# How a recurrence's operands reach TensorE: loads as the data lie and a spread by ScalarE, two chunks to a transpose, one buffer in another order

## The chip, the cores and the metric

The kernel runs on one core of one Trainium2 chip. The metric is the time of one execution on the device in microseconds (us), as a median of several runs. The engines are TensorE (PE, with its weight loads listed as PEld), VectorE (DVE), ScalarE (ACT), GpSimd (POOL) and SyncE (SP), whose queue issues nearly all DMAs of this kernel.

## The reference

One decoder layer over 2048 tokens of width 1024. After a norm and one input projection, two causal mixers run side by side: a diagonal state-space mixer, and RWKV-7 time mixing with 8 heads of 64. Their outputs are joined by an output projection, and a squared-ReLU MLP follows. The change touches the second mixer alone, whose recurrence the reference computes token by token:

```python
    def step(state, inp):
        r_t, d_t, k_t, v_t, kk_t, a_t = inp
        sa = jnp.einsum('bhvk,bhk->bhv', state, -kk_t)
        state = (state * d_t[:, :, None, :]
                 + sa[..., None] * (kk_t * a_t)[:, :, None, :]
                 + v_t[..., None] * k_t[:, :, None, :])
        return state, jnp.einsum('bhvk,bhk->bhv', state, r_t)
```

## The kernel before

The kernel does not step through tokens. It cuts the 2048 tokens into 32 chunks of 64, four chunks to a batch of 256 tokens, eight batches. Two heads share the 128 partitions, so there are four head pairs (`NP`), and a batch has four *units* and four *values*, one for each pair. The input phase leaves six operands for each pair and batch in DRAM, in `f_dram`, in the order k, v, b, a, q, bv, 256 numbers a partition each.

- `units` (L806) loads b and a of one pair into `ba`, a, q and k into `aq`, multiplies them chunk by chunk on TensorE (`ps_b` L817, `ps_a` L826) and evicts the products to `bQ` (VectorE L821, ScalarE L822) and `aR` (VectorE L827, ScalarE L828). `ba` holds a block diagonal: the first head's 64x64 block stands in the upper left, the second head's in the lower right, and the rest was set to zero once (L775). `load_pair` (L800) fills the two blocks straight from DRAM, one DMA for each half of the partitions, in runs of 64 numbers.
- After the fourth unit of a batch, `bQ`'s 32x32 diagonal blocks go to the DRAM buffer `abd` (L832), in the order row, quarter, block, column. `invert` (L861) reads them back as `M` (L865) with one block to a partition, inverts them in 62 small VectorE instructions (L876, L877) in `Z`, which GpSimd clears first (L868), and stores the result to `zd` (L880). `dtc` (L882) and, in `join` (L884), `lo` (L891) are read from `zd`.
- `values` (L834) does the same with k and v: `load_pair` fills `bk` with both as block diagonals, `ps_k` (L853) is multiplied, and `ps_v` (L851) holds four transposes, one for each chunk of v; because v lies on the diagonal, the transposed chunk is a block diagonal too, and one ScalarE copy (L855) takes all four to `vT`.
- `solve` (L908) makes `ps_pq`, evicts it with two ScalarE copies (L923, L924) to `pq`, and multiplies that into `ps_f` and `ps_h`. `chain` (L939) is the serial part: it takes `vT`, `hj`, `gf` and the state `S` through `ps_s` and stores the output rows `Y` (ScalarE L958).

In the main loop, one step handles one chunk of the chain, the solve of the chunk after next, one unit (13 ahead) and one value (5 ahead). TensorE's order is written out by hand there. The order on the other engines and on SyncE's queue is fixed when the kernel is built, by a planner that simulates the engines and takes instructions when their operands are ready in that simulation. Every engine then works through its queue in that order. The buffers `ba`, `aq`, `bk` and `qi` are there twice (`NB`), and `ps_k` and `ps_v` share one PSUM bank. The first two batches' units and inversions run beside the input phase, which ends at about 653 us.

Of the kernel before, what the change touches and what calls it, by code (L numbers as in the profile page):

```python
# [7 lines left out]
F32 = mybir.dt.float32  # L8
# [748 lines left out]
def rwkv_phase(K, f_dram, e_dram, n_dram, y_dram, ntok=2048):  # L757
# [7 lines left out]
    with ExitStack() as st:  # L765
# [5 lines left out]

        bas, aqs = [T([P, 2, NCH, P], f"ba{i}") for i in range(NB)], [T([P, 4, NCH, 64], f"aq{i}") for i in range(NB)]
        ist = c["ist"].rearrange("p (o x) -> p o x", o=1)
        for i in range(NB):
            g.memset(bas[i], 0.0)  # L775
            v.tensor_copy(aqs[i][:, 2], bc(ist, [P, NCH, 64]))
        S = None
# [3 lines left out]
        def begin(b):  # L781
            ub = uns[b % 4]
            B = dict(aR=ub.tile([P, NCH, NP, P], F32, tag="aR", name="aR"),
                     bQ=ub.tile([P, NCH, NP, 192], F32, tag="bQ", name="bQ"),
                     abd=K.dram.tile([32, 4, 16, 32], F32, tag="abd", bufs=3, name="abd"),
                     zd=K.dram.tile([32, 4, 16, 32], F32, tag="zd", bufs=3, name="zd"))

            nr, n2 = un.tile([NCH * NP, P], F32, tag="nr", name="nr"), ub.tile([P, NCH * NP], F32, tag="n2", name="n2")
            nc.sync.dma_start(out=nr, in_=n_dram[b * NCH:(b + 1) * NCH].rearrange("c t h s -> (c t) (h s)"))
            ps = pp("ps_nt")[:, 0:NCH * NP]  # L790
            pe.transpose(out=ps, in_=nr, identity=K.ident[0:NCH * NP, 0:NCH * NP])
            v.tensor_scalar(out=n2, in0=ps, scalar1=1e-24, scalar2=None, op0=ALU.max)
            v.reciprocal(out=n2, in_=n2)
            B["n2"] = n2
            return B
# [3 lines left out]

        def load_pair(t, b, p, o):  # L800

            for h in range(2):
                hp = slice(h * 64, h * 64 + 64)
                nc.sync.dma_start(out=t[hp, :, :, hp].rearrange("p n c x -> p (n c) x"), in_=f_dram[p, hp, b, o:o + 2].rearrange("p n (c x) -> p (n c) x", x=64))

        def units(b, B, p):  # L806

            aR, bQ = B["aR"], B["bQ"]
            i = (b * NP + p) % NB
            ba, aq = bas[i], aqs[i]  # L810
            load_pair(ba, b, p, RW["b"])
            nc.sync.dma_start(out=aq[:, 0:2].rearrange("p n c x -> p n (c x)"), in_=f_dram[p, :, b, RW["a"]:RW["a"] + 2])
            nc.sync.dma_start(out=aq[:, 3].rearrange("p c x -> p (c x)"), in_=f_dram[p, :, b, RW["k"]])
            for uu in range(0, NCH, 2):
                psb = pp("ps_b")
                for u in range(2):
                    pe.matmul(psb[:, u * 192:(u + 1) * 192], ba[:, 0, uu + u], aq[:, 0:3, uu + u], start=True, stop=True)  # L817
                for u in range(2):
# [6 lines left out]
            for u in range(NCH):  # L825
                pe.matmul(ps[:, u * P:(u + 1) * P], ba[:, 1, u], aq[:, 2:4, u], start=True, stop=True)  # L826
            v.tensor_tensor(out=aR[:, :, p, 0:64], in0=r4(ps)[:, :, 64:128], in1=mask(c["ma"], NCH), op=ALU.mult)  # L827
            act.copy(out=aR[:, :, p, 64:128], in_=r4(ps)[:, :, 0:64])  # L828
            if p == NP - 1:
                for hq in range(4):  # L830
                    q0 = (hq % 2) * 32
                    nc.sync.dma_start(out=B["abd"][:, hq], in_=bQ[hq * 32:(hq + 1) * 32, :, :, q0:q0 + 32].rearrange("s c p t -> s (c p) t"))  # L832

        def values(b, B, p):  # L834

            if p == 0:
                kv = kvs[b % 2]
                for n, shape in (("kT", [P, NCH, NP, P]), ("vT", [P, NCH, NP, P]), ("qS", [P, NP, TB])):
                    B[n] = kv.tile(shape, F32, tag=n, name=n)
                nc.sync.dma_start(out=B["qS"], in_=f_dram[:, :, b, RW["q"]].rearrange("t p n -> p t n"))  # L840
            kT, vT = B["kT"], B["vT"]
            i = (b * NP + p) % NB
            bk, qi = bks[i], qis[i]
            load_pair(bk, b, p, RW["k"])
            nc.sync.dma_start(out=qi[:, 0].rearrange("p c x -> p (c x)"), in_=f_dram[p, :, b, RW["q"]])
            for n in range(2):
                ps = pk("ps_" + "kv"[n])
                for u in range(NCH):
                    o = ps[:, u * P:(u + 1) * P]
                    if n:  # L850
                        pe.transpose(out=o, in_=bk[:, n, u], identity=K.ident)  # L851
                    else:
                        pe.matmul(o, bk[:, n, u], qi[:, :, u], start=True, stop=True)  # L853
                if n:
                    act.copy(out=vT[:, :, p], in_=r4(ps))  # L855
                else:
                    B["last"] = v.tensor_tensor(out=kT[:, :, p, 0:64], in0=r4(ps)[:, :, 0:64], in1=mask(c["mk"], NCH), op=ALU.mult)
                    act.copy(out=kT[:, :, p, 64:128], in_=r4(ps)[:, :, 64:128])
                    yield

        def invert(B, eng):  # L861

            M = un.tile([P, 32, 32], F32, tag="M", bufs=2, name="M")
            for par in range(2):
                nc.sync.dma_start(out=M[par * 64:par * 64 + 64], in_=B["abd"].rearrange("s q b t -> (q b) s t"))  # L865
            Z, prod = un.tile([P, 16, 32], F32, tag="Z", bufs=2, name="Z"), un.tile([P, 144], F32, tag="prod", name="prod")
            Zf = Z.rearrange("p i t -> p (i t)")
# [15 lines left out]

        def join(B):  # L884

            bQ, dtc = B["bQ"], B["dtc"]
            up, lo = (bt.tile([P, 16, 32], F32, tag=n, bufs=1, name=n) for n in ("up", "lo"))
            v.transpose(out=up.rearrange("p a t -> p (a t)"), in_=dtc.rearrange("p c a t -> p (c a t)"))
            halves = [(h, slice(h * 64, h * 64 + 32)) for h in range(2)]
            for h, hs in halves:  # L890
                nc.sync.dma_start(out=lo[hs].rearrange("s b t -> s (b t)"), in_=B["zd"][:, 2 * h + 1].rearrange("s b t -> s (b t)"))  # L891
            yield
# [86 lines left out]
        vp = pool(name="rwv", bufs=1)  # L979
        bks, qis = [T([P, 2, NCH, P], f"bk{i}", vp) for i in range(NB)], [T([P, 2, NCH, 64], f"qi{i}", vp) for i in range(NB)]  # L980
        for i in range(NB):
            g.memset(bks[i], 0.0)
            v.tensor_copy(qis[i][:, 1], bc(ist, [P, NCH, 64]))
        bt = pool(name="rwbt", bufs=2, side="right")
# [23 lines left out]
        with tc.manual_schedule(engines={mybir.EngineType.PE}):  # L1008
# [14 lines left out]

            for _ in join(Bs[0]):
                pass
# [721 lines left out]
```

## Time and profile before

| | |
|---|---|
| median of 3 runs | 2565.19 us (2565.0 to 2570.68) |
| profiled execution | 2566.72 us, its span 2565.0 us |
| TensorE busy | 2434.8 us, 95% of the span |
| VectorE, ScalarE, GpSimd busy | 1886.5, 1301.6 and 667.4 us (74%, 51%, 26%) |
| mean granted TensorE clock | 0.979 of full speed |
| recurrence with the hand-written order | about 655 to 965 us of the span |

Times in the rows count from the span's first instruction. A row of a timeline gives start, duration, engine, line, operation, output and inputs, and in brackets how long the engine idled before and what ended that. A busy TensorE is not one at its peak, since the ends of its matmuls are modelled and overlap; where a price of a matmul is needed, the distance between starts is the better figure. SPq is SyncE issuing DMAs.

### The profile page before, as it was taken

How to read it: one execution, taken by the hardware profiler on the slowest of the kernel's cores; microseconds unless marked ns; L12 is line 12 of the kernel's file. 1: busy time of each engine (PE TensorE's matmuls, PEld its weight loads, DVE VectorE, ACT ScalarE, POOL GpSimd, SP SyncE). 2: the span in 40 equal slices, each digit the busy share in tenths (PEclk: the TensorE clock that was granted, in tenths of full speed). 3: DMA queues.
4: the chain of work that ended last, by engine and by line, in shares of the span. 5: the costliest groups of instructions: out<-in, count | busy, mean ns of one | idle time of the engine just before them, and what ended most of it. 6: DMA issues, size and time to landing. Idle time of an engine off the chain costs nothing.

```text
span 2565.0 us, 38224 instructions
## 1 busy us (share of the span) xinstructions
PE 2434.8 (95%) x13084; PEld 2020.9 (79%) x13084; DVE 1886.5 (74%) x3326; ACT 1301.6 (51%) x2555; POOL 667.4 (26%) x662
## 2 busy tenths in 40 slices
PE   7999989999898998999899999999989999999998
PEld 6987667787798987888688888888867778877786
DVE  7558897579687868766777668877757777666777
ACT  6355545465454446555476666666653333333334
POOL 1058798711322223231033230322310000000001
PEclk9999989999899998999999999999999999999999
DMA  9656747997777636443457555766577555455545
GB/s 288 214 166 180 223 120 218 255 259 180 182 161 160 137 88 222 145 155 125 160 205 251 208 191 199 239 209 214 186 265 283 187 182 169 161 175 181 169 158 195
DMA packets 541266, 491.49 MB, mean 192 GB/s; under 512 B 187312, under 2 KB 442800, under 8 KB 541072
## 3 DMA queue, kind: packets, MB, share of 16 engines
q1 hardware_dynamic: 539360, 483.54, 60.7%
q0 software_dynamic: 992, 3.67, 0.5%
q8 instruction: 104, 1.70, 0.3%
q10 hardware_dynamic: 720, 1.84, 0.2%
q14 instruction: 90, 0.74, 0.1%
HBM read 303.23 MB, written 180.49 MB: 189 GB/s over the span
## 4 chain that ended last, share of the span: by engine, by line
PE 70%; DVE 12%; DMA 9%; ACT 3%; issue 2%; POOL 2%; SPq 1%; DVEq 0%; POOLq 0%; ACTq 0%
PE ps_ua L1328 13%; PE ps_da L1328 11%; PE ps_ux L1328 7%; PE ps_dx L1328 5%; PE ps_ub L1328 3%; PE ps_db L1328 3%; PE ps_o L433 2%; PE ps_o L435 2%; PE ps_o L434 2%; DMA wraw<-in_w_down 2%; PE ps_z L433 1%; PE ps_z L434 1%; PE ps_z L435 1%; DMA wr<-in_w_in 1%; DVE acc L1620 1%
## 5 line engine op out<-in xcount | busy, mean ns | idle before, releaser
L1624 ACT COPY c<-ps_da 128x512 f32<-128x512 f32 x192 | 106.3, 588 | 259.1 <-PE ps_da L1328 256.9
L1620 DVE TENSOR_TENSOR acc<-acc,c 128x512 f32<-128x512 f32 x192 | 127.3, 689 | 105.0 <-ACT c L1624 104.8
L433 PE MATMUL ps_z<-xh,wh 128*128 128x512 f32 x448 | 184.8, 413 | 16.9 <-DVE zr L617 7.1
L435 PE MATMUL ps_z<-xh,wl 128*128 128x512 f32 x448 | 182.1, 407 | 0.0
L434 PE MATMUL ps_z<-xl,wh 128*128 128x512 f32 x448 | 181.5, 405 | 0.0
L386 POOL TENSOR_TENSOR frs<-frs,mhalf 128x1 f32<-128x1 f32 x16 | 10.4, 650 | 645.0 <-DVE frs L385 645.0
L1425 DVE TENSOR_TENSOR wl<-wraw,wh 128x512 fp32r<-128x512 f32 x124 | 104.4, 843 | 28.2 <-ACT wh L1424 27.9
L433 PEld LDWEIGHTS ps_z<-xh,wh 128*128 128x128 f32 x448 | 87.5, 195 | 41.7 <-DVE zr L617 8.9
L374 ACT CAST hh<-hr 128x512 fp32r<-128x512 f32 x96 | 59.6, 621 | 110.2 <-PE ps_da L1328 81.5
L609 DVE TENSOR_TENSOR wl<-wr,wh 128x1024 fp32r<-128x1024 f32 x56 | 86.1, 1537 | 35.7 <-ACT wh L608 35.4
L433 PE MATMUL ps_o<-woh,ys 128*128 128x512 f32 x256 | 103.0, 403 | 2.5 <-DVE xrow L1225 2.5
L1424 ACT CAST wh<-wraw 128x512 fp32r<-128x512 f32 x124 | 76.1, 616 | 52.8 <-PE ps_ua L1328 34.1
L435 PEld LDWEIGHTS ps_z<-xh,wl 128*128 128x128 f32 x448 | 87.4, 195 | 19.4 <-issue 0.5
L434 PEld LDWEIGHTS ps_z<-xl,wh 128*128 128x128 f32 x448 | 87.6, 196 | 18.7 <-issue 0.9
L434 PE MATMUL ps_o<-wol,ys 128*128 128x512 f32 x256 | 102.1, 400 | 0.0
L435 PE MATMUL ps_o<-woh,ys 128*128 128x512 f32 x256 | 100.7, 396 | 0.0
L913 POOL TENSOR_TENSOR DT<-dtc,cst 128x128 f32<-128x128 f32 x128 | 56.2, 470 | 159.8 <-PE ps_pq L920 107.2
L1291 POOL TENSOR_TENSOR ws<-wraw 128x512 f32<-128x512 f32 x28 | 41.2, 1471 | 200.9 <-DMA hs_d<-hh 72.7
L1474 DVE TENSOR_TENSOR hh<-hs,hh 128x512 fp32r<-128x512 f32 x96 | 79.7, 830 | 14.5 <-ACT hh L1473 13.5
L1620 DVE TENSOR_TENSOR acc<-acc,ps_dx 128x512 f32<-128x512 f32 x128 | 87.5, 684 | 2.9 <-PE ps_dx L1328 1.1
L1473 ACT CAST hh<-hs 128x512 fp32r<-128x512 f32 x96 | 59.7, 622 | 58.4 <-DVE hs L1490 21.3
L1425 DVE TENSOR_TENSOR wl<-ws,wh 128x512 fp32r<-128x512 f32 x93 | 66.8, 721 | 30.5 <-ACT wh L1424 26.0
(693 smaller groups left out, 8159.2 us busy)
## 6 DMA issues: line engine op xcount, KB each, us to landing
hs_d<-hh SPq DMA_DIRECT2D x256, 256.0 KB
hs<-hs_d SPq DMA_DIRECT2D x126, 512.0 KB
wraw<-in_w_up SPq DMA_DIRECT2D x62, 512.0 KB
wr<-in_w_in SPq DMA_DIRECT2D x56, 512.0 KB
hr<-hr_d SPq DMA_DIRECT2D x94, 256.0 KB
hr_d<-c SPq DMA_DIRECT2D x93, 256.0 KB
xrow<-in_x SPq DMA_DIRECT2D x32, 512.0 KB
wraw<-in_w_down SPq DMA_DIRECT2D x14, 1024.0 KB
```

The costliest lines, as they stand in the source:

```text
L374: nc.scalar.copy(out=hi, in_=raw)
L433: K.nc.tensor.matmul(out, lh, rh, start=i == 0, stop=False)
L434: K.nc.tensor.matmul(out, lh, rl, start=False, stop=False)
L435: K.nc.tensor.matmul(out, ll, rh, start=False, stop=i == n - 1)
L609: v.tensor_tensor(out=wl, in0=wr, in1=wh.bitcast(F32), op=ALU.subtract)
L1328: K.nc.tensor.matmul(ps, a[k], b[k], start=start and k + i == 0, stop=k == n - 1 and i == 2, skip_group_check=True)
L1424: act.copy(out=hi, in_=o)
L1425: v.tensor_tensor(out=lo, in0=o, in1=hi.bitcast(F32), op=ALU.subtract)
L1473: act.copy(out=hi, in_=o)
L1474: v.tensor_tensor(out=lo, in0=o, in1=hi.bitcast(F32), op=ALU.subtract)
L1620: add = lambda eng, o, s: eng.tensor_tensor(out=o, in0=o, in1=s, op=ALU.add)
L1624: act.copy(out=t, in_=ps)
```

## The change

Operands are loaded as they lie in DRAM, in whole rows: for a unit b, a and q in one DMA and k in another, into `fu`; for a value k and v in one and q in another, into `fv`. The two blocks of the diagonal are then written by two ScalarE copies (`spread`), into `ba` for a unit and into `bk` (now k alone) for a value. v is transposed from `fv`, two chunks to a transpose; the blocks come out beside each other, and four small ScalarE copies put them into `vT`, whose zeros are set once by GpSimd at the start. The buffer `abd` is stored in the order quarter, block, row, column, so that `M` reads 4 KB runs; the store's side in DRAM becomes runs of 128 bytes. `Z` has one buffer where it had two. The load of `lo` is issued at the end of the previous batch's `join`, for the batch after.

```diff
-        bas, aqs = [T([P, 2, NCH, P], f"ba{i}") for i in range(NB)], [T([P, 4, NCH, 64], f"aq{i}") for i in range(NB)]
+        bas, fus = [T([P, 2, NCH, P], f"ba{i}") for i in range(NB)], [T([P, 5, NCH, 64], f"fu{i}") for i in range(NB)]
...
-                     abd=K.dram.tile([32, 4, 16, 32], F32, tag="abd", bufs=3, name="abd"),
+                     abd=K.dram.tile([4, 16, 32, 32], F32, tag="abd", bufs=3, name="abd"),
...
-        def load_pair(t, b, p, o):
+        def spread(t, src):
 
             for h in range(2):
                 hp = slice(h * 64, h * 64 + 64)
-                nc.sync.dma_start(out=t[hp, :, :, hp].rearrange("p n c x -> p (n c) x"), in_=f_dram[p, hp, b, o:o + 2].rearrange("p n (c x) -> p (n c) x", x=64))
+                act.copy(out=t[hp, ..., hp], in_=src[hp])
...
-            ba, aq = bas[i], aqs[i]
-            load_pair(ba, b, p, RW["b"])
-            nc.sync.dma_start(out=aq[:, 0:2].rearrange("p n c x -> p n (c x)"), in_=f_dram[p, :, b, RW["a"]:RW["a"] + 2])
-            nc.sync.dma_start(out=aq[:, 3].rearrange("p c x -> p (c x)"), in_=f_dram[p, :, b, RW["k"]])
+            ba, fu = bas[i], fus[i]
+            nc.sync.dma_start(out=fu[:, 0:3].rearrange("p n c x -> p n (c x)"), in_=f_dram[p, :, b, RW["b"]:RW["b"] + 3])
+            nc.sync.dma_start(out=fu[:, 4].rearrange("p c x -> p (c x)"), in_=f_dram[p, :, b, RW["k"]])
+            spread(ba, fu[:, 0:2])
...
-                    nc.sync.dma_start(out=B["abd"][:, hq], in_=bQ[hq * 32:(hq + 1) * 32, :, :, q0:q0 + 32].rearrange("s c p t -> s (c p) t"))
+                    nc.sync.dma_start(out=B["abd"][hq].rearrange("b s t -> s b t"), in_=bQ[hq * 32:(hq + 1) * 32, :, :, q0:q0 + 32].rearrange("s c p t -> s (c p) t"))
...
-            bk, qi = bks[i], qis[i]
-            load_pair(bk, b, p, RW["k"])
-            nc.sync.dma_start(out=qi[:, 0].rearrange("p c x -> p (c x)"), in_=f_dram[p, :, b, RW["q"]])
+            bk, fv = bks[i], fvs[i]
+            nc.sync.dma_start(out=fv[:, 0:2].rearrange("p n c x -> p n (c x)"), in_=f_dram[p, :, b, RW["k"]:RW["k"] + 2])
+            nc.sync.dma_start(out=fv[:, 2].rearrange("p c x -> p (c x)"), in_=f_dram[p, :, b, RW["q"]])
+            spread(bk, fv[:, 0])
...
-                        pe.transpose(out=o, in_=bk[:, n, u], identity=K.ident)
...
-                    act.copy(out=vT[:, :, p], in_=r4(ps))
+
+                    for e in range(0, NCH, 2):
+                        pe.transpose(out=ps[:, e * 64:e * 64 + P], in_=fv[:, 1, e:e + 2].rearrange("p c x -> p (c x)"), identity=K.ident)
+                    for h in range(2):
+                        hp = slice(h * 64, h * 64 + 64)
+                        for e in range(2):
+                            act.copy(out=vT[hp, e::2, p, hp], in_=ps[e * 64:e * 64 + 64, 0:2 * P].rearrange("p (c x) -> p c x", c=2)[:, :, hp])
...
-                nc.sync.dma_start(out=M[par * 64:par * 64 + 64], in_=B["abd"].rearrange("s q b t -> (q b) s t"))
-            Z, prod = un.tile([P, 16, 32], F32, tag="Z", bufs=2, name="Z"), un.tile([P, 144], F32, tag="prod", name="prod")
+                nc.sync.dma_start(out=M[par * 64:par * 64 + 64], in_=B["abd"].rearrange("q b s t -> (q b) s t"))
+            Z, prod = un.tile([P, 16, 32], F32, tag="Z", bufs=1, name="Z"), un.tile([P, 144], F32, tag="prod", name="prod")
...
+        def load_lo(B):
+            B["lo"] = bt.tile([P, 16, 32], F32, tag="lo", bufs=1, name="lo")
+            for h, hs in halves:
+                nc.sync.dma_start(out=B["lo"][hs].rearrange("s b t -> s (b t)"), in_=B["zd"][:, 2 * h + 1].rearrange("s b t -> s (b t)"))
+
+        def join(B, after):
...
-            for h, hs in halves:
-                nc.sync.dma_start(out=lo[hs].rearrange("s b t -> s (b t)"), in_=B["zd"][:, 2 * h + 1].rearrange("s b t -> s (b t)"))
+            if "lo" not in B:
+                load_lo(B)
+            lo = B["lo"]
...
+            if after is not None:
+                load_lo(after)
...
+        vTs = [T([P, NCH, NP, P], "vT", kvs[i]) for i in range(2)]
+        for t in vTs:
+            g.memset(t, 0.0)
...
-                    jn = join(Bs[b + 1])
+                    jn = join(Bs[b + 1], Bs.get(b + 2))
```

## Rows read from the trace of the kernel before

**Rows 1.** Busy time of each engine by stretch, then granted clock, DMA share, GB/s.

```profile
560.00:650.00 90.00, 83.21 (x373) 64.65 (x371) 81.08 (x184) 49.57 (x110) 12.97 (x11) 1.00 0.75 185
...
655.00:965.00 310.00, 283.54 (x2971) 275.10 (x2969) 228.68 (x770) 140.64 (x336) 80.71 (x210) 0.95 0.65 145
```

**Rows 2.** Waits of TensorE, 655 to 965: us in total, times, longest.

```profile
PE ps_k L853 <- DMA lo<-zd: 8.1, 2, 4.3
...
PE ps_f L928 <- ACT pq L924: 4.8, 6, 1.2
...
PE ps_b L817 <- DMA ba<-f_d: 4.1, 1, 4.1
...
PE ps_k L853 <- ACT bQ L822: 3.0, 1, 3.0
...
PE ps_k L853 <- DMA bk<-f_d: 2.1, 2, 1.9
...
PE ps_k L853 <- DMA qi<-f_d: 1.6, 1, 1.6
```

**Rows 3.** Timeline, SyncE's queue at a batch's end: start, us, instruction [idle before].

```profile
760.60 2.05 SPq L832 DMA_DIRECT2D abd<-bQ  x4
...
765.58 2.72 SPq L865 DMA_DIRECT2D M<-abd  x2
...
771.35 1.28 SPq L804 DMA_DIRECT2D bk<-f_d  x2
...
772.67 1.08 SPq L891 DMA_DIRECT2D lo<-zd  x2
```

**Rows 4.** Timeline, TensorE and GpSimd in the same place.

```profile
770.97 0.60 PE L851 MATMUL ps_v<-cst,bk 128*128 128x128 f32 x4
...
771.41 0.39 PE L949 MATMUL ps_s<-vT,hj 128*128 128x128 f32 x2
...
778.51 1.13 PE L853 MATMUL ps_k<-qi,bk 128*128 128x128 f32 x8 [3.85 <-DMA lo<-zd]
...
776.64 1.70 POOL L913 TENSOR_TENSOR DT<-dtc,cst 128x128 f32<-128x128 f32 x4 [6.06 <-DMA dtc<-zd]
```

**Rows 5.** DMA, columns as in rows 1: with M's load, without it; packets.

```profile
764.00:776.00 12.00, 10.66 (x89) 10.37 (x87) 7.23 (x26) 4.93 (x14) 2.97 (x9) 1.00 0.96 167
...
784.00:796.00 12.00, 12.00 (x195) 11.72 (x194) 11.25 (x39) 6.57 (x15) 1.84 (x4) 1.00 0.52 142
...
DMA packets 129687, 44.93 MB, mean 145 GB/s; under 512 B 112779, under 2 KB 123355, under 8 KB 129648
```

**Rows 6.** Stretches of 10 us after the waits, columns as in rows 1.

```profile
780.00:790.00 10.00, 10.00 (x119) 9.84 (x119) 8.05 (x25) 4.36 (x9) 1.84 (x4) 0.84 0.59 154
...
820.00:830.00 10.00, 8.55 (x50) 8.59 (x51) 6.80 (x22) 3.07 (x9) 1.50 (x4) 0.66 0.55 142
...
860.00:870.00 10.00, 7.03 (x45) 6.76 (x45) 7.20 (x26) 3.47 (x10) 1.76 (x4) 0.83 0.78 200
...
900.00:910.00 10.00, 6.97 (x37) 6.56 (x36) 7.38 (x27) 2.16 (x5) 1.77 (x4) 0.66 0.53 130
```

**Rows 7.** Groups of ScalarE by line, 655 to 965: count, busy, mean ns, idle before.

```profile
L855 ACT COPY vT<-ps_v 128x512 f32<-128x512 f32 x32 | 18.8, 587 | 27.2 <-PE ps_v L851 27.0
...
L924 ACT COPY pq<-ps_pq 64x512 f32<-64x512 f32 x31 | 18.0, 580 | 0.8
```

**Rows 8.** Timeline, ScalarE and TensorE around the solve's eviction.

```profile
717.12 0.36 ACT L958 COPY Y<-ps_s 64x256 f32<-64x256 f32 x1 [1.23 <-DVE S L957]
...
718.00 0.58 ACT L924 COPY pq<-ps_pq 64x512 f32<-64x512 f32 x1
...
718.73 1.06 PE L928 MATMUL ps_f<-bQ,pq 128*128 128x128 f32 x8
```

**Rows 9.** Chain that ended last, at the hand-over: start, us, what.

```profile
658.98 0.90 POOL bk L982
...
660.53 3.20 DMA bk<-f_d
```

More of the change, by code (lines that the diff above doesn't have):

```diff
@@ L775, in rwkv_phase @@
             g.memset(bas[i], 0.0)
-            v.tensor_copy(aqs[i][:, 2], bc(ist, [P, NCH, 64]))
+            v.tensor_copy(fus[i][:, 3], bc(ist, [P, NCH, 64]))
         S = None
@@ L816, in units @@
                 for u in range(2):
-                    pe.matmul(psb[:, u * 192:(u + 1) * 192], ba[:, 0, uu + u], aq[:, 0:3, uu + u], start=True, stop=True)
+                    pe.matmul(psb[:, u * 192:(u + 1) * 192], ba[:, 0, uu + u], fu[:, 1:4, uu + u], start=True, stop=True)
                 for u in range(2):
@@ L825, in units @@
             for u in range(NCH):
-                pe.matmul(ps[:, u * P:(u + 1) * P], ba[:, 1, u], aq[:, 2:4, u], start=True, stop=True)
+                pe.matmul(ps[:, u * P:(u + 1) * P], ba[:, 1, u], fu[:, 3:5, u], start=True, stop=True)
             v.tensor_tensor(out=aR[:, :, p, 0:64], in0=r4(ps)[:, :, 64:128], in1=mask(c["ma"], NCH), op=ALU.mult)
@@ L837, in values @@
                 kv = kvs[b % 2]
-                for n, shape in (("kT", [P, NCH, NP, P]), ("vT", [P, NCH, NP, P]), ("qS", [P, NP, TB])):
+                for n, shape in (("kT", [P, NCH, NP, P]), ("qS", [P, NP, TB])):
                     B[n] = kv.tile(shape, F32, tag=n, name=n)
+                B["vT"] = vTs[b % 2]
                 nc.sync.dma_start(out=B["qS"], in_=f_dram[:, :, b, RW["q"]].rearrange("t p n -> p t n"))
@@ L882, in invert @@
             nc.sync.dma_start(out=B["dtc"].rearrange("p c a t -> p (c a t)"), in_=B["zd"].rearrange("s q b t -> q s (b t)"))
-        def join(B):
+        halves = [(h, slice(h * 64, h * 64 + 32)) for h in range(2)]
+        def load_lo(B):
[3 more added lines that the diff above has]
+        def join(B, after):
             bQ, dtc = B["bQ"], B["dtc"]
-            up, lo = (bt.tile([P, 16, 32], F32, tag=n, bufs=1, name=n) for n in ("up", "lo"))
+            up = bt.tile([P, 16, 32], F32, tag="up", bufs=1, name="up")
             v.transpose(out=up.rearrange("p a t -> p (a t)"), in_=dtc.rearrange("p c a t -> p (c a t)"))
-            halves = [(h, slice(h * 64, h * 64 + 32)) for h in range(2)]
-            for h, hs in halves:
-                nc.sync.dma_start(out=lo[hs].rearrange("s b t -> s (b t)"), in_=B["zd"][:, 2 * h + 1].rearrange("s b t -> s (b t)"))
+            if "lo" not in B:
+                load_lo(B)
+            lo = B["lo"]
             yield
@@ L979, in rwkv_phase @@
         vp = pool(name="rwv", bufs=1)
-        bks, qis = [T([P, 2, NCH, P], f"bk{i}", vp) for i in range(NB)], [T([P, 2, NCH, 64], f"qi{i}", vp) for i in range(NB)]
+        bks, fvs = [T([P, NCH, P], f"bk{i}", vp) for i in range(NB)], [T([P, 4, NCH, 64], f"fv{i}", vp) for i in range(NB)]
+        vTs = [T([P, NCH, NP, P], "vT", kvs[i]) for i in range(2)]
+        for t in vTs:
+            g.memset(t, 0.0)
         for i in range(NB):
             g.memset(bks[i], 0.0)
-            v.tensor_copy(qis[i][:, 1], bc(ist, [P, NCH, 64]))
+            v.tensor_copy(fvs[i][:, 3], bc(ist, [P, NCH, 64]))
         bt = pool(name="rwbt", bufs=2, side="right")
@@ L1022, in solution @@
                 return solve(Bs[n // NCH], n % NCH) if n < nb * NCH else none
-            for _ in join(Bs[0]):
+            for _ in join(Bs[0], Bs[1]):
                 pass
```

7 lines of the change are left out of this document (2 added, 5 removed).

## The prediction

> **What bounds the kernel now.** I read the stretches first, then the waits of the engine that is busiest there, then the timeline at those waits. The change lies in the recurrence. In its own stretch, 655 to 965 us, TensorE is busy 283.5 of 310 us, VectorE 228.7, ScalarE 140.6 [rows 1]: TensorE is the bound, and 26.5 us are its idle time. Before that, beside the end of the input phase, TensorE is busy 83.2 of 90 us and VectorE 81.1 [rows 1]; only two of eight batches' units run there, so I look for little in it.
>
> The waits of TensorE in the recurrence [rows 2] are of two kinds. Late operands make 18.9 us: 8.1 (named lo), 4.1 (ba), 3.0 (named bQ, but the matmul waiting is ps_k, which reads only bk and qi, and bQ had been evicted), 2.1 (bk) and 1.6 (qi). ScalarE's eviction of pq makes 4.8 us in six short waits. The timeline shows how the first kind arises, about once in a batch. The four stores of abd start at 760.60, the two loads of M are issued at 765.58, and bk's load comes out only at 771.35, just after the transposes that free its buffer (770.97) but also behind all of that in one queue; lo follows at 772.67, and the next ps_k starts at 778.51 after 3.85 us of idleness [rows 3, 4]. So bk and lo need up to 5.8 us from the end of bk's issue (772.63) to use, while a bk load elsewhere lands in 3.20 us [rows 9]. The stretch with M's load has a DMA share of 0.96, the one without it 0.52 [rows 5]. By the code M is read in 4096 pieces of 128 bytes a batch, and b, a, k and v in 2048 pieces of 256 bytes a step: of the 129,687 packets in the recurrence 112,779 are under 512 bytes [rows 5].
>
> After four of these waits the granted clock falls: 0.84, 0.66, 0.83 and 0.66 over 10 us [rows 6], that is part of each stretch at 1.2 instead of 2.4 GHz. At full speed those 40 us would hold 1.6 + 3.4 + 1.7 + 3.4 = 10.1 us less.
>
> **The change part by part.** *Transposes.* Four transposes of a value start at 770.97 and the next matmul at 771.41 [rows 4]: 0.44 us, 0.11 each. Two remain, so 0.22 us less in each of 32 values, **7.0 us**, all on the engine that is the bound.
>
> *Late operands.* M's load shrinks from 4096 pieces to 128 a batch, a unit's from 1280 to 256 (two halves of 512 pieces of b and a, 256 rows of aq, to 256 rows), a value's from 1152 to 256. Issues in the queue fall from four to two for a unit and from three to two for a value. At the place in rows 3 M's issue takes 2.72 us for two and bk's 1.28 for two; I take some 3 us off the queue ahead of bk, and 2.6 off its landing (5.8 to 3.2). Against that stands the spread of bk, 0.72 us (two copies at the 0.36 of the 64x256 copy of Y, [rows 8]), and lo, which may now be issued beside dtc and so ahead of bk, 1.08 us [rows 3]. Some 4 us gained stand against single waits of 1.6 to 4.3 us. All 18.9 would be the upper end. What is late next is DT on GpSimd: it waits for dtc until 776.64 and takes 1.70 us [rows 4], which is close to where TensorE would be without the wait. I take 13 of the 18.9, **13 us**; the lower end is nothing.
>
> *Clock.* With the waits the falls should go; I take 6 of 10.1, **6 us**, with ends 0 and 10.1.
>
> *ScalarE's new work.* A unit's spread writes 512 numbers a partition twice, at 0.58 us each (the 64x512 copy of pq, [rows 7, 8]): 1.16 us. A value's spread is 0.72 us. The four vT copies write 128 numbers each; from 0.36 us for 256 and 0.58 for 512 [rows 8], 128 would take 0.25, so 4 x 0.25 = 1.0 against 0.587 now [rows 7], 0.41 more. For 24 units and 32 values in the stretch: 27.8 + 36.2 = 64 us, ScalarE from 141 to 205 of 310 us. It has room, so the price is only what comes between ps_pq and ps_f. There the cover is thin: the second copy of pq starts at 718.00, takes 0.58, and ps_f starts at 718.73 [rows 8], 0.15 us later. But ScalarE idled 1.23 us just before, waiting for VectorE's S [rows 8], and a spread that falls there costs nothing. Its buffer is freed by ps_a or ps_k of two steps before, so it has most of a step of about 10 us in which to go. The ends are 0 (more instructions in the queue can gain nothing by themselves) and one unit's spread in the way in each of 28 steps, 32.5 us. With 169 us of idle time against 64 us added, I take a fifth of that upper end, **minus 6 us**.
>
> *Small parts.* In the input phase eight units bring ScalarE 9.3 us more, beside VectorE, which is the fuller engine there; fewer pieces help M's first load. I count 0, with ends of 5 us better and 9 worse. At the hand-over the load of bk waits for GpSimd's clearing of bk (658.98, 0.90 each) and then takes 3.20 us [rows 9]. Afterwards the loads need not wait, and it is the spread that does, but GpSimd has two tiles vT of 2048 numbers to clear, 3.6 us by the price of bk's 1024, and half as much for bk. The two cancel: 0. Z's single buffer makes GpSimd wait for zd's store before it clears, with DT behind it; inversions are some 40 us apart, so 0, and up to DT's 1.70 us a batch if that cover is gone.
>
> The sum is -7 - 13 - 6 + 6 = **-20 us**: the profiled execution from 2566.7 to 2546.7, and the median, 1.5 us below that execution, from 2565.2 to **2545**.
>
> **The rivals.** *ScalarE is held by loads (slower).* A spread stands at a fixed place of ScalarE's queue, and nothing there waits for a DMA in the recurrence today. Where a load lands later than the planner thought, the evictions of ps_s, ps_pq and ps_b behind the spread wait, and TensorE with them. If a load is late by the difference seen above, 2.6 us, less the 1.23 us of idle time, a step loses 1.4 us: 32 steps make 45 us, and 2565 - 26 + 45 = 2584. It decides from 26 / 32 = 0.8 us a step. For it speaks the thin cover [rows 8]; against it that the loads become fewer and larger, and that a buffer is freed a step ahead.
>
> *The waits stay (no change).* M is loaded only when abd's stores have landed, 765.58 against 760.60 to 762.65 for their issue [rows 3], and M holds the queue in which bk stands. If the stores, now scattered in DRAM, land some 3 us later, what M's load gives is lost again, and the clock falls stay too. Then 7 is gained and 6 lost: 2564. A sentence of the Trainium skill speaks for this rival: the page DMA: Bandwidth & Descriptors, section Specifications, gives 512 bytes as the least transfer for full rate and says that the engine reads, modifies and writes below that; abd's runs in DRAM fall from 2048 bytes to 128. By that rule each batch's store would slow down, and the time would be this rival's; no row of before shows such a store, and against it stands that the source side was in pieces of 128 bytes all along.
>
> *The change does not do what it says.* If TensorE's steps were set by the chain of S through VectorE, fewer transposes would only lengthen idle time. TensorE without any idle time in most stretches between the waits, as 12.00 of 12 us [rows 5], speaks against it; I give it no share of its own.
>
> **How the numbers follow.** The forecast has 0.75, with a range of its own from 2565 - 36 (all of 7.0, 18.9 and 10.1, nothing on ScalarE) = 2529 to 2557. The waits that stay have 0.14, ScalarE held has 0.11. About 0.3%, or 7.7 us, is what a measurement of this kernel can tell from no change. The range of 8 in 10 goes from 2523, for a gain in the input phase too, to 2567, past the rival without change; it leaves out ScalarE held and some of each end. Faster 0.75, same 0.14, slower 0.11.
>
> **What would show it.** In the changed kernel, TensorE's stretch should shrink from 310 to about 290 us; the transposes should number two a value, 0.11 us apart; ps_k's waits for DMAs should be mostly gone and M's issue should be short; the granted clock should stay at 1.00 between 700 and 900 us; ScalarE should be busy some 205 us there, with waits of its spreads for f_dram near 0. Wrong would be: waits of ScalarE for fu or fv of several tens of us and ps_f waiting for pq in every step (first rival), or ps_k waiting as before behind a late M (second).

## The result, and the profile of the changed kernel

The changed kernel takes 2587.59 us (median of 4 runs, 2584.19 to 2589.9) against 2565.95 for the kernel before beside it: a ratio of 1.0072, 95% interval 1.0056 to 1.0088 (the two medians alone give 1.0084). It is slower by some 19 to 22 us; the forecast was 2545. What came is the rival "ScalarE is held by loads", in sign and, by luck as will be seen, nearly in size (2584).

**Where the time went.** Three landmarks on TensorE place it: the first ps_x, which opens the recurrence, moved from 654.0 to 658.4 us; the first ps_o, after the recurrence, from 1002.4 to 1026.0; the first ps_ua, in the MLP, from 1256.4 to 1279.2. So 4.4 us were lost before the recurrence, 19.2 in it (348.4 us became 367.6), and nothing behind it. The recurrence as a whole, before and, below, after, columns as in [rows 1]:

```profile
654.00:1002.40 348.40, 312.03 (x3164) 300.21 (x3165) 263.75 (x842) 166.76 (x388) 96.97 (x222) 0.94 0.67 158
658.40:1026.00 367.60, 317.46 (x3092) 303.32 (x3092) 264.39 (x844) 230.91 (x592) 97.70 (x226) 0.91 0.52 142
```

Busy time of each engine by stretch after the change, in the stretches of [rows 1]:

```profile
560.00:650.00 90.00, 86.97 (x394) 68.06 (x392) 78.60 (x178) 56.15 (x125) 10.48 (x10) 1.00 0.62 171
655.00:965.00 310.00, 269.51 (x2715) 258.26 (x2716) 226.35 (x764) 192.77 (x512) 77.49 (x201) 0.92 0.51 135
```

In the same 310 us TensorE now gets through 2715 matmuls instead of 2971 (68 of the 256 are transposes that the change saves), at a granted clock of 0.92 instead of 0.95, while ScalarE rises from 140.64 us to 192.77 and the DMA share falls from 0.65 to 0.51. The loads are fewer and lighter, as the change meant, and the stretch is longer.

Waits of TensorE, 655 to 990 us (us in total, times, longest), which answer to [rows 2]:

```profile
PE ps_k L861 <- ACT vT L858: 12.9, 6, 3.8
PE ps_f L942 <- ACT pq L938: 10.7, 11, 3.9
PE ps_b L818 <- ACT up L911: 8.0, 5, 2.5
...
PE ps_b L818 <- ACT bQ L823: 2.6, 1, 2.6
PE ps_a L827 <- ACT aR L829: 2.4, 1, 2.4
```

None of the recurrence's loads is left among them, as the prediction wanted. But where TensorE waited for loads it now waits for ScalarE's copies of vT, pq, up, bQ and aR. The next view tells why: ScalarE's own waits and, below, its groups by line (count, busy, mean ns, idle before).

```profile
ACT bk L805 <- DMA fv<-f_d: 25.8, 15, 4.8
ACT vT L858 <- PE ps_v L854: 12.9, 13, 2.0
ACT ba L805 <- PE ps_a L827: 11.9, 7, 2.8
...
ACT ba L805 <- DMA fu<-f_d: 7.5, 5, 2.5
```

```profile
L858 ACT COPY vT<-ps_v 64x128 f32<-64x128 f32 x128 | 33.3, 260 | 14.2 <-PE ps_v L854 12.9
...
L805 ACT COPY ba<-fu 64x512 f32<-64x512 f32 x44 | 27.1, 616 | 22.4 <-PE ps_a L827 11.9 <-DMA fu<-f_d 7.5 <-issue 1.5
L805 ACT COPY bk<-fv 64x256 f32<-64x256 f32 x64 | 25.8, 403 | 28.8 <-DMA fv<-f_d 25.8 <-POOL bk L999 1.8
```

In 15 of 32 values ScalarE stands at the spread of bk until fv's load has landed, 25.8 us together. In one place on the timeline (start, us, instruction, idle before it and until what):

```profile
865.65 0.38 PE L854 MATMUL ps_v<-cst,fv 128*128 128x128 f32 x2
...
869.04 1.11 SPq L870 DMA_DIRECT2D M<-abd  x2
870.26 1.33 SPq L885 DMA_DIRECT2D zd<-Z  x2
...
871.40 0.37 ACT L863 COPY kT<-ps_k 128x256 f32<-128x256 f32 x1
871.64 1.96 SPq L977 DMA_DIRECT2D y_d<-Y  x1
...
873.63 0.58 SPq L846 DMA_DIRECT2D fv<-f_d  x1
...
873.77 0.38 PE L854 MATMUL ps_v<-cst,fv 128*128 128x128 f32 x2
...
876.58 0.83 ACT L805 COPY bk<-fv 64x256 f32<-64x256 f32 x2 [4.81 <-DMA fv<-f_d]
...
878.39 1.24 ACT L805 COPY ba<-fu 64x512 f32<-64x512 f32 x2 [0.98 <-DMA fu<-f_d]
...
879.64 0.37 ACT L829 COPY aR<-ps_a 128x256 f32<-128x256 f32 x1
...
879.91 1.07 ACT L858 COPY vT<-ps_v 64x128 f32<-64x128 f32 x4
...
881.04 2.07 PE L861 MATMUL ps_k<-fv,bk 128*128 128x128 f32 x8 [3.79 <-ACT vT L858]
```

The ps_v of 873.77 was there at 874.15, and its copies could have started then. ScalarE had run out of earlier work at 871.77 and stood at bk's spread until 876.58; the vT copies came out at 879.91 behind the two spreads and aR. The spread of bk is for the next value, and so is the ps_k that waited for those copies, because it shares its PSUM bank with ps_v: TensorE stood still for 3.79 us. After this pause, and after one of 3.86 us before a ps_f at 924.97, the granted clock was low for a while; two stretches of 10 us show it (columns as in [rows 6]):

```profile
880.00:890.00 10.00, 8.96 (x55) 8.96 (x56) 6.77 (x24) 7.05 (x22) 1.70 (x4) 0.66 0.45 121
920.00:930.00 10.00, 6.14 (x43) 5.95 (x43) 7.86 (x26) 3.45 (x9) 1.72 (x4) 0.83 0.37 96
```

Over the whole recurrence the mean granted clock went from 0.94 (654.0 to 1002.4) to 0.91 (658.4 to 1026.0). What is missing to full speed is 348.4 x 0.06 = 20.9 us before and 367.6 x 0.09 = 33.1 us after: some 12 us more are clock (the two rounded means leave 1.8 us of play on each). TensorE's idle time grew by 13.8 us, from 348.4 - 312.0 = 36.4 to 367.6 - 317.5 = 50.1. The transposes take 6.9 us off, and so the three make the 19.2 within that play.

### The profile page after: what moved, and what is told of

It is laid out like the page before. It is cut to its first block, busy times and chain, and to the rows that moved or that the text cites. A ratio compares the mean times of both kernels' runs of the same rounds, so it can differ in the third digit from the quotient of the medians.

```text
span 2588.1 us, 38252 instructions
## 1 busy us (share of the span) xinstructions
PE 2442.0 (94%) x13020; PEld 2026.3 (78%) x13020; DVE 1889.6 (73%) x3326; ACT 1376.2 (53%) x2779; POOL 669.6 (26%) x664
## 2 busy tenths in 40 slices
DMA packets 446546, 487.28 MB, mean 188 GB/s; under 512 B 87472, under 2 KB 342960, under 8 KB 446352
## 4 chain that ended last, share of the span: by engine, by line
PE 68%; DVE 13%; DMA 7%; ACT 5%; issue 4%; POOL 2%; SPq 1%; DVEq 0%; POOLq 0%; ACTq 0%
PE ps_ua L1345 13%; PE ps_da L1345 11%; PE ps_ux L1345 7%; PE ps_dx L1345 5%; PE ps_ub L1345 3%; PE ps_db L1345 3%; PE ps_o L433 2%; PE ps_o L434 2%; PE ps_o L435 2%; DMA wraw<-in_w_down 2%; PE ps_z L433 2%; PE ps_z L434 1%; PE ps_z L435 1%; DVE acc L1637 1%; PE ps_f L942 1%
## 5 line engine op out<-in xcount | busy, mean ns | idle before, releaser
L386 POOL TENSOR_TENSOR frs<-frs,mhalf 128x1 f32<-128x1 f32 x16 | 10.4, 652 | 643.9 <-DVE frs L385 643.9
L1441 ACT CAST wh<-wraw 128x512 fp32r<-128x512 f32 x124 | 76.1, 616 | 51.2 <-PE ps_ua L1345 36.4
L1491 DVE TENSOR_TENSOR hh<-hs,hh 128x512 fp32r<-128x512 f32 x96 | 79.0, 823 | 12.7 <-ACT hh L1490 10.7
L1441 ACT CAST wh<-ws 128x512 fp32r<-128x512 f32 x93 | 57.3, 617 | 53.2 <-PE ps_ua L1345 31.8
```

Source lines behind the costliest of these rows:

```text
L1441: act.copy(out=hi, in_=o)
L1491: v.tensor_tensor(out=lo, in0=o, in1=hi.bitcast(F32), op=ALU.subtract)
```

## The experiments

Each ratio is to the kernel before on the same chip, whose median there was 2571.4 to 2572.5 us, with its 95% interval; 0.1% is 2.6 us. "Recurrence" is the time from the first ps_x to the first ps_o in the profiled execution: 348.4 us before, 367.6 after the change. Each run is a build of its own, in which the planner orders the queues anew, so a run can differ from another in more than its edit. Four theories were on trial: *holding* (ScalarE waits at a spread for a load), *work* (the added copies by themselves), *queue* (y's store at the head of SyncE's queue makes the loads late), and the *other parts* (Z's single buffer, lo's place, abd's order).

**The spreads taken out.** The changed kernel with b, a and k loaded into the diagonals again, one DMA for each half in runs of 64 numbers.

```diff
-            spread(ba, fu[:, 0:2])
+            pair(ba, b, p, RW["b"], 2)
...
-            spread(bk, fv[:, 0])
+            pair(bk, b, p, RW["k"], 1)
```

> The changed kernel with its two diagonals, ba and bk, loaded from DRAM by halves again as before; the paired transposes with their four vT copies, abd's order, Z's one buffer and the early load of lo stay. Theory H (ScalarE stands at a spread whose load or buffer comes late, 25.8 + 7.5 us behind loads and 11.9 behind ps_a in the trace of after, and the evictions behind it make TensorE wait): with no spreads the time falls below that of before, to some 2550 us (2540 to 2560). Theory W (ScalarE's added busy time is too much by itself): the same here. Theory O (the loss comes from Z's one buffer, abd's scattered store or lo's place): stays near the 2587 of after, 2578 or more.

Measured: 1.0014 (1.0003 to 1.0024). The spreads cost about 0.58%, 15 us. But what is left of the change is no gain either, which none of the theories had expected.

**The same work, nothing to wait for.** On top of that, ScalarE makes copies of the same shapes from a constant into a scratch tile, in the program where the spreads were: one for each half in units, and the shorter ones in values.

```diff
+                act.copy(out=scr[hp], in_=K.cst[hp, 0:512])
...
+                act.copy(out=scr[hp, 0:256], in_=K.cst[hp, 0:256])
```

> e_load plus ScalarE copies of the same shapes as the spreads (two of 64x512 a unit, two of 64x256 a value), from a constant tile to a scratch tile that nobody reads: the same work on ScalarE, but never a wait for a load or a buffer. Theory H: within 8 us of e_load. Theory W: near the 2587 of after, at least 20 us above e_load.

Measured: 1.0032 (1.0016 to 1.0048), 0.18% above the run without the copies, and the two intervals overlap. This run doesn't part work from holding, because the added copies were not made in the recurrence. Since they wait for nothing, they ran early (count, shortest, median and longest in ns, first and last start):

```profile
L825 ACT COPY scr<-cst x64: 602/617/624, 508.5 to 635.6; 64x512 f32<-64x512 f32 x64
L862 ACT COPY scr<-cst x64: 387/402/408, 529.7 to 650.3; 64x256 f32<-64x256 f32 x64
```

In the recurrence ScalarE is as busy as without them, 180.35 us against 180.34, and the recurrence takes 353.6 us against 354.4; it begins 3.3 us later. What the work by itself costs is left to the run with a third buffer, below.

**Another engine holds.** The spreads on GpSimd.

```diff
-                act.copy(out=t[hp, ..., hp], in_=src[hp])
+                g.tensor_copy(t[hp, ..., hp], src[hp])
```

> The changed kernel with the spreads done by GpSimd instead of ScalarE. ScalarE then has neither the work nor the waits; GpSimd, 81 of 310 us busy in the recurrence, has them. Theory H: the evictions are free again, 2550 to 2565, unless GpSimd held at a spread makes DT late, which would show as TensorE waiting for DT and a time of 2575 to 2600. Theory W: 2550 to 2565. Theory O: 2578 or more with TensorE still waiting for ScalarE.

Measured: 1.0079 (1.0063 to 1.0095), no better than the change. TensorE now waits 6.8 us for bk and 4.0 for ba from GpSimd, and still 10.0 for pq (655 to 965). Moving the spread moves the wait.

**abd's order alone.** The kernel before with abd stored in runs for M's load.

```diff
-                     abd=K.dram.tile([32, 4, 16, 32], F32, tag="abd", bufs=3, name="abd"),
+                     abd=K.dram.tile([4, 16, 32, 32], F32, tag="abd", bufs=3, name="abd"),
```

> The kernel before with abd's order alone changed. Step of the prediction: M's load in runs takes late operands away, some 5 to 15 us, 2550 to 2560. Rival of the scattered store (in O): abd lands later, ps_k waits as before, 2562 to 2580.

Measured: 0.9995 (0.9985 to 1.0005), no change. Its waits of TensorE, 655 to 965, beside [rows 2]:

```profile
PE ps_k L853 <- DMA lo<-zd: 10.3, 3, 4.2
PE ps_k L853 <- DMA bk<-f_d: 5.7, 2, 5.5
PE ps_b L817 <- DMA ba<-f_d: 4.6, 1, 4.6
```

M's issue became shorter (2.00 us for the two, where [rows 3] have 2.72), and the waits stayed. The stores of abd were not late enough to hold it up: M's load was issued 5.17 us after the first of them (764.04 to 769.21), 4.98 before (760.60 to 765.58). So the rule of the Trainium skill that the prediction weighed (page DMA: Bandwidth & Descriptors, section Specifications) does not decide here in either direction: packets under 512 bytes fell from 187,312 to 154,544 in the whole run, and the time is the same.

**Which spread.** One of the two loaded again, the other left to ScalarE: first bk's taken out, then ba's.

```diff
-            spread(bk, fv[:, 0])
+            pair(bk, b, p, RW["k"], 1)
```

> The changed kernel with the values' k loaded into its diagonal by halves again, and the units' b and a still spread by ScalarE. Places the loss between the two spreads, 15 us together. Theory 'held where it is late': the spread of bk carries 25.8 of the 33.3 us for which ScalarE is held, so some 11 of the 15 us go with it, and the time is about 7 us above the kernel before. Rival 'the work': the spread of ba is the longer one (616 against 403 ns), and if the work counts rather than the holding only some 6 us go: 12 us above the kernel before.

```diff
-            spread(ba, fu[:, 0:2])
+            pair(ba, b, p, RW["b"], 2)
```

> The changed kernel with the units' b and a loaded into the diagonals by halves again, and the values' k still spread by ScalarE. The other half of the pair with the run that loads k into its diagonal: that one was at the time of the kernel before (0.9998), so the spread of ba costs nothing there and the spread of bk some 18 us. Theory 'bk's spread by itself': that cost is there without ba's spread as well, and the time is 15 to 22 us above the kernel before. Rival 'the two together': ScalarE is only short of time where it has both to do; then the time is 4 to 10 us above the kernel before, near the run with both diagonals loaded (3.6 us above).

Measured: without bk's spread 0.9998 (0.9987 to 1.0008), recurrence 349.1 us; without ba's 1.0086 (1.0071 to 1.0101), recurrence 363.3 us. By these two runs all of the loss hangs on the spread of bk, though it is the shorter copy. And holding ScalarE need not cost anything. In the run without bk's spread it is held at ba's longer than it had been at bk's:

```profile
ACT ba L805 <- DMA fu<-f_d: 32.5, 9, 5.8
```

and that run is at the time of the kernel before. In the run without ba's, bk's spread waits 34.6 us, and TensorE, behind the vT copies,

```profile
PE ps_k L869 <- ACT vT L866: 23.6, 6, 7.3
```

For the copies of vT, which stand behind the spread in ScalarE's queue, TensorE waits 23.6 us here and 10.4 in the run without bk's spread. That it stands less behind ba's spread is what the rows show; why, no run here takes apart.

**The queue.** The changed kernel, and then the kernel before, with y's store issued from ScalarE's queue, where it has nothing to wait for. In the changed kernel SyncE stands 47.2 + 29.6 us at this store, for pq's and Y's copies.

```diff
-            nc.sync.dma_start(out=y_dram[t0:t0 + 64], in_=yS)
+            nc.scalar.dma_start(out=y_dram[t0:t0 + 64], in_=yS)
```

> The changed kernel with one edit: the store of a chunk's output y is issued from ScalarE's queue instead of SyncE's. ScalarE itself writes what is stored, so the store waits for nothing there, and SyncE's queue no longer stands at it (in the changed kernel SyncE waits there 47.2 us for pq's copies and 29.6 us for Y's copies between 655 and 990). Theory 'loop': the loads of fu and fv are late because they stand behind this store in SyncE's queue, and the store waits for ScalarE, which is itself held at a spread by the load before. Then ScalarE's waits at the spreads (25.8 + 7.5 us) fall under 10 us and the time falls by 8 to 15 us against the changed kernel: 5 to 12 us above the kernel before on this chip. Rival 'buffers': a load can't start before its buffer's last reader is done, two steps earlier, whatever stands before it in the queue. Then the waits at the spreads stay near 30 us and the time stays within 3 us of the changed kernel, about 18 to 22 us above the kernel before.

> The kernel before with the same one edit: the store of y is issued from ScalarE's queue. Theory 'loop': in the kernel before, too, the loads that came late at a batch's end stood behind this store. Then TensorE's waits for bk, ba and qi (5 + 4 + 2 us of the recurrence's batched part) and the clock dips behind them go, and the time is 6 to 12 us under the kernel before. Rival 'buffers': no change, within 3 us, and these waits are still there.

Measured: 1.0083 (1.0068 to 1.0098) and 0.9995 (0.9985 to 1.0005): no gain in either, and the "loop" theory falls. With the store gone SyncE stands longer at the loads themselves, for the last readers of their buffers (the changed kernel, 655 to 990):

```profile
SPq L812 <- PE ps_b L818: 50.3, 13, 8.9
SPq L847 <- PE ps_k L861: 39.6, 19, 9.1
SPq L846 <- PE ps_v L854: 39.0, 15, 7.8
```

The store is only a part of what stands in that queue, and the rest was not moved in any run. The trace of the changed kernel shows what the rest does, when the start of each load of fv is set against the end of ps_v two values before, the last reader of its buffer. Of 30 loads 16 left the queue at most 0.24 us after that, and ScalarE waited for two of them, 1.0 us together. The other 14 left it 0.7 to 7.6 us after, and the other 24.9 us of ScalarE's wait are for 13 of those. Nearly all of these come around a batch's end, behind abd's stores, M's loads (and their wait for abd), zd's stores or the loads of dtc and lo. The place shown with the result is the worst: ps_v was through with the buffer at 866.03, and the load of fv started at 873.63, behind M, zd and y. With y's store moved the same load is still 5.4 us late, behind M and zd. So the large waits at bk's spread are made, as far as the trace tells, by the queue at a batch's end; a build with the loads of fv ahead of M, or with M in another queue, was not tried.

**A third buffer.** The changed kernel with three buffers of fv, so that a load can start a step earlier; room comes from one buffer of M instead of two. First with y's store moved as well, then without.

```diff
-            bk, fv = bks[i], fvs[i]
+            bk, fv = bks[i], fvs[(b * NP + p) % 3]
...
-            M = un.tile([P, 32, 32], F32, tag="M", bufs=2, name="M")
+            M = un.tile([P, 32, 32], F32, tag="M", bufs=1, name="M")
```

> The changed kernel with a third buffer for the values' operands as they lie (room for it made by one buffer for M instead of two), and y's store issued from ScalarE's queue. With y's store alone moved, SyncE stood at the loads of fv for 39.0 + 39.6 us until the matmuls that read the buffer two steps earlier were done, and ScalarE's wait at bk's spread stayed (31.3 us). Theory 'holding': with a third buffer the load starts a step earlier, the waits of ScalarE at bk's spread fall under 10 us, and most of the 18 us go: 2 to 8 us above the kernel before. Rival 'the work in its place': the two copies of 403 ns a step stand ahead of what TensorE waits for, whether the load is there or not. Then ScalarE's waits fall but the time stays 15 to 22 us above.

> The changed kernel with a third buffer for the values' operands as they lie and one buffer for M, and y's store on SyncE's queue as it was. Theory 'buffers alone': the load of fv no longer waits for the matmuls two steps back, ScalarE is hardly held at bk's spread, and the time is within 4 us of the run that also moved y's store, -2 to +3 us to the kernel before. Rival 'both are needed': y's store, which waits for ScalarE, keeps the loads behind it late; ScalarE's waits at bk's spread stay over 15 us and the time is 8 to 20 us above the kernel before.

Measured: 0.9992 (0.9979 to 1.0005) with the store moved, 1.0008 (0.9995 to 1.0021) with the buffer alone; the recurrence takes 347.7 and 346.5 us. All the work of the spreads is still there (with the buffer alone ScalarE is busy 228.9 us in the recurrence, where the changed kernel has 230.9), and the loss is gone. ScalarE's waits at the spreads, with the buffer alone:

```profile
ACT ba L805 <- DMA fu<-f_d: 12.7, 6, 4.0
...
ACT bk L805 <- DMA fv<-f_d: 3.0, 5, 0.9
```

25.8 us became 3.0, while SyncE stands at y's store as long as ever (45.9 + 30.1 us). So the buffer does it, and the place of y's store does not matter. The load that was 7.6 us late in the changed kernel now starts at 842.24, 0.03 us after its buffer is free and ahead of that batch's abd and M (848.38 and 852.19): with a third buffer the loads get into the queue before a batch's end fills it. This is the run that settles the cause as far as it goes: the work of the spreads does not cost the time, standing at bk's spread for late loads does.

The way from there to TensorE is only in part as the timeline suggested. TensorE's idle time in the recurrence falls to 346.5 - 307.3 = 39.2 us and its mean granted clock rises to 0.93, but it still waits 9.1 us for vT and 14.0 for pq (12.9 and 10.7 in the changed kernel); gone are its waits for ScalarE's up (8.0) and bQ (2.6), while one for kT grew (0.9 to 4.3).

**The paired transposes alone.** The kernel before with v loaded as it lies, two transposes and four ScalarE copies a value; then the same with vT cleared after bk's buffers instead of before; then the first one with two of the four copies on VectorE.

```diff
+                    for e in range(0, NCH, 2):
+                        pe.transpose(out=ps[:, e * 64:e * 64 + P], in_=fv[:, 0, e:e + 2].rearrange("p c x -> p (c x)"), identity=K.ident)
...
+                                v.tensor_copy(vT[hp, e::2, p, hp], src)
```

> The kernel before with one part of the change alone: v is loaded as it lies and transposed two chunks at a time, four ScalarE copies of 64x128 take the place of one of 128x512, and vT is cleared once. Diagonals of b, a and k are loaded, the order of the inverses' operand, Z's two buffers and the place of lo's load are as before. Theory 'the pairing pays': 64 transposes of 0.11 us less, 7 us, less 3 us for the clears of vT at the hand-over: 4 us under the kernel before. Rival 'the copies eat it': four copies take 1.07 us on ScalarE where one took 0.59, and pq's copies stand behind them: 0 to 4 us above the kernel before, with TensorE's waits for pq near 8 us instead of 4.8.

> The kernel before with the paired transposes alone, as in the run that was at 0.9989, but with vT cleared after the buffers of bk instead of before them. In that run the recurrence began 3.2 us later than in the kernel before (657.2 against 654.0) and took 2.1 us less. Theory 'clears': bk's first load waited for bk's clear behind vT's on GpSimd (1.81 us each, the second held until 662.15); with the order changed the recurrence begins at 654 to 655, and the time is 5 to 7 us under the kernel before. Rival 'other': the later start has another cause; then it stays at 657, and the time 2 to 4 us under.

> The kernel before with the paired transposes alone, and of the four copies of a value's vT the two for the second head on VectorE instead of ScalarE. Theory 'the copies eat it': with four copies on ScalarE TensorE waited 10.7 us for pq's copies and 4.8 us for up's (4.9 and 1.2 in the kernel before); with half of them gone from ScalarE these fall back by 4 to 8 us, and the time is 5 to 10 us under the kernel before. Rival 'never there': the waits fall, but TensorE's clock or another wait takes the time; the time stays 0 to 4 us under the kernel before.

Measured: 0.9989 (0.9978 to 1.0001), 0.9997 (0.9983 to 1.0011) and 1.0005 (0.9995 to 1.0015). No difference clear of noise in any of them. TensorE's rows of the transposes in the kernel before and, below, in the first of these runs (655 to 1000 us; count, busy, mean ns):

```profile
L851 PE MATMUL ps_v<-cst,bk 128*128 128x128 f32 x128 | 19.3, 274 | 0.2
```

```profile
L862 PE MATMUL ps_v<-cst,fv 128*128 128x128 f32 x64 | 12.4, 276 | 0.0
```

The saving is there, 6.9 us of TensorE's time, but the recurrence is only 2.1 us shorter (346.3 against 348.4) and begins 3.2 us later. Within it idle time grew from 36.4 to 346.3 - 307.7 = 38.6 us, and busy time fell by 4.4 us instead of 6.9, at a mean granted clock of 0.93 instead of 0.94. TensorE waits less for loads there, and more for ScalarE, 655 to 990 (4.9 us for pq and 1.2 for up in the kernel before, 654 to 1002):

```profile
PE ps_f L948 <- ACT pq L944: 10.7, 12, 2.3
...
PE ps_b L826 <- ACT up L919: 4.8, 4, 1.8
```

With half of the copies on VectorE the wait for pq is still 13.1 us. So it isn't settled that the four copies alone make it longer. The clears of vT are not what started the recurrence late: it began at 657.9 us with their order changed, 657.2 without. The last fq of the input phase on GpSimd was late by the same 3.2 us already (646.51 against 643.29), and an early one by 3.6 (179.46 against 175.91), long before the recurrence. What makes it late stays open.

**Two attempts at a faster version.** What had cost nothing, together: ba spread by ScalarE, k loaded, paired transposes, Z with two buffers and lo loaded in join; and the version with a third buffer and y's store moved, with two of the four vT copies on VectorE.

```diff
-            Z, prod = un.tile([P, 16, 32], F32, tag="Z", bufs=1, name="Z"), ...
+            Z, prod = un.tile([P, 16, 32], F32, tag="Z", bufs=2, name="Z"), ...
...
-            if after is not None:
-                load_lo(after)
```

> What the runs so far leave over of the change: units' b and a loaded as they lie and spread by ScalarE, k loaded into its diagonal, v loaded as it lies and transposed two chunks at a time, vT cleared after bk; Z has two buffers and lo is loaded in join again, as in the kernel before. Theory 'Z and lo': with both diagonals loaded, one buffer of Z and lo's early load cost the difference between the run of the pairing alone (0.9989) and the run with both diagonals loaded (1.0014), 6 us; here, on top of the run with k loaded (0.9998), they come back, and 3 us from the clears: 6 to 10 us under the kernel before. Rival 'they cost nothing where ba is spread': 0 to 4 us under.

> The version with a third buffer and y's store on ScalarE's queue (2 us under the kernel before), with the second head's copies of vT on VectorE. Theory 'the copies eat it': TensorE's waits for vT and pq (9.3 + 10.1 us) fall by half, and the time is 7 to 14 us under the kernel before. Rival 'never there': 0 to 5 us under.

Measured: 1.0005 (0.9995 to 1.0015) and 1.0022 (1.0013 to 1.0031). In the first the recurrence took 345.0 us, 3.4 less than before, but began 3.1 us later. In the second TensorE waits 6.0 us for vT and 6.1 for Z from VectorE, and 12.0 for pq, where it waited 10.1 without the last edit. No version is under the kernel before by more than the measurement can tell.

## Why the prediction was wrong

*What bounds the kernel* held: the loss is all in TensorE's idle time and clock. The failing steps are among the terms.

*ScalarE's new work, -6 us.* This is the step that failed most. Its sizes were right: 1.24 us for a unit's spread, 0.83 for a value's and 1.07 for the four copies, against 1.16, 0.72 and 1.0. Failing was the reason that a spread has "most of a step of about 10 us in which to go", because its buffer is freed two steps before. That looks at the buffer that the spread writes. What sets it is the load that it reads: fv's load can start only after ps_v of two values before, at a batch's end it started up to 7.6 us later than that, behind M and zd in SyncE's queue, and the spread stands in ScalarE's queue ahead of copies that TensorE waits for. In the kernel before the same lateness met ps_k alone. In place of -6 the term was some -15, by the run with the spreads taken out, to -21, by the third buffer (1.0072 to 1.0008 or 0.9992, 16 to 21 us).

The rival's lateness was right in kind, but wrong in extent: it had 1.4 us in each of 32 steps, and 15 steps had 1.7 on average, with clock on top. That it gave nearly the measured time is luck: it set 45 us of loss against 26 us of gains, and the runs show 15 to 21 us of loss and next to none of the gains.

*Late operands, 13 us, and clock, 6 us.* Both came to nothing. That M's 4096 pieces make the loads late is refuted by the run with abd's order alone: waits and clock stayed. That y's store does is refuted too, on the kernel before as well. The queue itself is not refuted, and the prediction read its own rows wrongly there. It took the transposes of 770.97 [rows 4] for the ones that free the buffer of bk's load at 771.35 [rows 3]. Those belong to the value just before. With two buffers, bk's load needs the transposes of two values before, which are earlier:

```profile
762.98 0.60 PE L851 MATMUL ps_v<-cst,bk 128*128 128x128 f32 x4
```

They were over at 763.58, so the load stood 7.8 us behind others in the queue, and after the change the load of the same value still stood there 6.3 us (777.60 to 783.92): fewer and shorter issues took little off. In the changed kernel TensorE's waits for DMAs did go, but into ScalarE's waits for the same loads, and the clock's falls stayed with them. No run shows what the kernel before would gain from earlier loads; the third buffer that helped the changed kernel was not tried there.

*Transposes, 7.0 us.* The size was right (6.9 us in the stretch). That it would reach the end was not: in the run with this part alone 2.1 us reached the end of the recurrence, idle time and clock took the rest, and the later start took the 2.1. TensorE's waits for pq and up grew by 5.8 + 3.6 us. "All on the engine that is the bound" is no sufficient reason, when that engine idles for another one in the same step.

*Input phase 0 and hand-over 0.* The recurrence began 4.4 us later, within the ends of -9 to +5 that were kept for the input phase; the other builds began 0 to 7.5 us later, so part of this differs from build to build. The clears of vT, where I had looked for it, were not the cause.

*Z's single buffer and lo, 0.* With both diagonals loaded the recurrence took 354.4 us, with the pairing alone 346.3. Between them are Z, lo and abd, and abd alone is nothing. So they may cost some 8 us there, though the third buffer's run has both and takes 346.5; open.

*The rivals and chances.* Signs in the list of what would show it were well chosen: waits of the spreads for fv of several tens of us came as the sign of the first rival. What was wrong is its chance of 0.11. The late loads that it needed stood in [rows 2 to 4] already: TensorE waited for them, and ScalarE, whose copy has to come before TensorE's use, waited for longer, 25.8 us, which is the 0.8 us a step that the prediction had named as the point where this rival decides.

## What to carry to other kernels

A copy on an in-order engine between a load and its user does not inherit the user's slack: it stands in that engine's queue, and everything behind it waits for the load. Before such a copy goes in, count the buffers on the side that it reads, and set each load's start against the end of its buffer's last reader: what lies between them is the queue. Here a third buffer was worth 16 to 21 us, while fewer pieces, shorter issues and another queue for y's store were worth nothing. And look in the trace where an experiment's added work has landed: copies that wait for nothing ran before the stretch that they were to load. Read a late load in the kernel before as a warning for it, not as a gain to come.

## What the runs showed of the hardware that I had not expected

Holding has no fixed price: 32.5 us of ScalarE held at ba's spread cost nothing, 25.8 us at bk's spread cost some 19 (1.0072 against 0.9998). And the number of small pieces had no bearing on the time here: the changed kernel moves 87,472 packets under 512 bytes, the kernel before 187,312, the version with the third buffer alone moves 87,473 and takes the time of the kernel before. A 64x512 copy from SBUF takes ScalarE 616 ns, 6% longer than one of the same shape from PSUM (580).
